# One Strassen level in the up projection of a gated feed-forward, and the gated result kept in DRAM

## The chip, the cores and the metric

The kernel runs on one core of one Trainium2 chip. The metric is device time in microseconds of one execution; times below are medians of separate runs, and the trace is that of one further, profiled execution.

## The reference

An encoder layer is applied with the same weights to 256 prompt tokens and 1024 sample tokens (D = 1024, all float32). The first half (projections, retention, pooling, memory attention, merge, output projection, residual) isn't touched by the change. The second half is a gated feed-forward with a depthwise convolution over the tokens:

```python
h2 = rmsnorm(x, g_ffn_pre)
u = h2 @ w_up                      # 1024 -> 2 * 2816
u = conv(u, conv_w) + conv_b       # centred, width 3, per channel, per group of tokens
gate, val = split(u)
x = x + rmsnorm((gelu(gate) * val) @ w_down, g_ffn_post)
```

The convolution never reaches from prompt tokens to sample tokens.

## The kernel before

Every float32 operand of a matmul is split in two reduced-precision (`fp32r`) parts: `hilo` lets ScalarE copy the high part and VectorE subtract it from the source to get the low part. `mm3` then issues three matmuls: high x high, high x low, low x high. So each product costs three matmuls, and each operand one ScalarE copy and one VectorE subtraction.

`Weights` is the stream of weight units (128 x 1024) through SBUF in the order of a list. SP loads a unit into one of two raw buffers (`wr`), `split_to` splits it into a ring of four pairs `wh`, `wl`, and the buffer's next load is issued then, when the buffer has been read. `take` hands units out and splits ahead up to the ring's limit; `tick` loads and splits when there is room.

Instructions run on each engine in the order in which the program writes them. `bg` is a list of background generators (closing a tile of the output projection, for example); `step` advances each by one piece, so a piece stands in the engines' queues where the main loop calls `step`.

After the output projection (order written out by hand over 10 token tiles and 8 blocks; `finish` writes normalized, transposed activations to DRAM as `h2_d`), the feed-forward runs twice, once for each half of the 1280 tokens. In each half:

- Up: for each of the 22 blocks m of 128 channels, the gate and the value unit of `w_up` are taken. The half's tokens come in two groups (256 + 386 columns in the first, 322 + 322 in the second; the excess columns are neighbours that the convolution needs). Each group and unit is 8 x 3 matmuls into a bank `f`. `conv` reads the bank: ScalarE the centre tap with bias into `z`, VectorE the two outer taps. ScalarE applies GELU and VectorE multiplies gate and value into `gs[m]`, which stays in SBUF.
- Down: 44 steps n, each with the split `gl` of one `gs` block held as TensorE's weights for five token tiles and 512 columns of `w_down` moving.

So `w_up` is read twice. GpSimd does no arithmetic in these stages; it only issues stores. Its queue and SP's are in order too.

Of the kernel before, what the change touches and what calls it, by code (L numbers as in the profile page):

```python
# [8 lines left out]
F32 = mybir.dt.float32  # L9
# [48 lines left out]
class Weights:  # L58
    RAW, RING = 2, 4

    def __init__(self, nc, pool, srcs):
        self.nc, self.pool, self.srcs = nc, pool, srcs
        self.raw, self.hl = {}, {}
        self.n_load = self.n_split = self.n_taken = self.n_done = 0
        self.limit = self.load_limit = len(srcs)

    def load(self):
# [16 lines left out]
    def split_to(self, h, l):  # L84
        r = self.raw.pop(self.n_split)
        self.nc.scalar.activation(h, r[:], AF.Copy)  # L86
        self.nc.vector.tensor_tensor(out=l, in0=r[:], in1=h.bitcast(F32), op=ALU.subtract)  # L87
        self.n_split += 1
        self.load()
# [20 lines left out]
def encoder(ctx: ExitStack, tc: tile.TileContext, a: dict):  # L110
# [3 lines left out]
    dram = ctx.enter_context(tc.tile_pool(name="scratch", bufs=1, space=DRAM))  # L114
    wpool = ctx.enter_context(tc.tile_pool(name="w", bufs=1))
    big = ctx.enter_context(tc.tile_pool(name="big", bufs=1))
# [72 lines left out]
    srcs += [a["w_ret_out"][i] for i in range(8)]  # L189
    srcs += [a["w_o"][i] for i in range(8)]  # L190
    for _ in range(2):
        for p in range(NF):
            srcs += [a["w_up"][p], a["w_up"][NF + p]]
        srcs += [a["w_down"][i] for i in range(NF)]
    ws = Weights(nc, wpool, srcs)
    wo_at = len(srcs) - 2 * 3 * NF - KC
    ws.limit = wo_at
# [27 lines left out]
    x2_d = [dram.tile([P, D], F32, name=f"x2d{i}") for i in range(NT)]  # L225
    h2_d = dram.tile([P, KC, T], F32, name="h2d")

    bg = []
# [702 lines left out]

    slots["bx"] = ctx.enter_context(tc.tile_pool(name="bx", bufs=1))
    op = ctx.enter_context(tc.tile_pool(name="outp", bufs=1))
# [105 lines left out]

    lp = accs.enter_context(tc.tile_pool(name="lhs", bufs=1))  # L1040

    def finish(t, bs, x):
# [23 lines left out]
        for hf in range(2):  # L1066
            b = fbank()[:].rearrange("p (a b) -> p a b", b=P)
            for i in range(4):
                c = 4 * hf + i
                nc.tensor.transpose(b[:, i, :], v[:, c * P:(c + 1) * P], ident[:])  # L1070
            s = op.tile([P, 4, P], F32, tag="h2s", name="h2s", bufs=2)
            nc.scalar.activation(s, b, AF.Copy)
            nc.gpsimd.dma_start(out=h2_d[:, 4 * hf:4 * hf + 4, t * P:(t + 1) * P], in_=s[:])
            yield

    def h2_raw(c, base, r):
        w = min(642, T - base)
        nc.sync.dma_start(out=r[:, 0:w], in_=h2_d[:, c, base:base + w])
        return r[:, 0:w], w

    def h2_split(c, raw):
        r, w = raw
        if c % 2 == 0:
            hx.append(slot([2, 2, 642]))
        s = hx[c // 2]
        hilo(r, s[:, c % 2, 0, 0:w], s[:, c % 2, 1, 0:w], col("g_ffn_pre", c))

    def wraw():
        return wpool.tile([P, 1024], F32, tag="wr", name="wr", bufs=Weights.RAW)

# [22 lines left out]
    for n in range(LA):  # L1113
        acc_split(n)
    hx = []
    raw = {}
    for n, (t, c) in enumerate(order):
# [11 lines left out]
        if t == 0:  # L1129
            if c in (0, 1):  # L1130
                late_merge(c + 1)
            elif c in (2, 3):
                wo += load_wo(1)
            elif c == 4:
                ws.limit = len(srcs)
# [6 lines left out]
        pos = (t - 7) * KC + c  # L1142
        sched = {6: 0, 8: 1, 10: 2, 12: 3, 18: 4, 19: 5, 21: 6, 22: 7}
        if pos in (4, 5):
            raw[pos - 4] = h2_raw(pos - 4, 0, wraw())
        if pos in sched:
            k = sched[pos]
            h2_split(k, raw.pop(k))
            if k + 2 < KC:
                raw[k + 2] = h2_raw(k + 2, 0, wraw())  # L1150
    ws.load_limit = len(srcs)
    accs.close()

    fp = ctx.enter_context(tc.tile_pool(name="ffn", bufs=1))
    gpost2 = []
    halves = (
        (0, 0, ((0, 256, 0, 256), (256, 386, 256, 384))),
        (638, 640, ((639, 322, 640, 320), (958, 322, 960, 320))),
    )

    def conv(b, s, n, o, m, u, first, last):
        z = fp.tile([P, 384], F32, tag=f"z{u}", name="z", bufs=2)
        wi = 3 * (u * NF + m)
        ce = o - s
        nc.scalar.activation(z[:, 0:n], b[:, ce:ce + n], AF.Identity, scale=col("conv_w", wi + 1),  # L1165
                             bias=col("conv_b", u * NF + m))
        l = 1 if first else 0
        nc.vector.scalar_tensor_tensor(out=z[:, l:n], in0=b[:, ce + l - 1:ce + n - 1], scalar=col("conv_w", wi),  # L1168
                                       in1=z[:, l:n], op0=ALU.mult, op1=ALU.add)
        r = n - 1 if last else n  # L1170
        nc.vector.scalar_tensor_tensor(out=z[:, 0:r], in0=b[:, ce + 1:ce + 1 + r], scalar=col("conv_w", wi + 2),  # L1171
                                       in1=z[:, 0:r], op0=ALU.mult, op1=ALU.add)
        return z

# [31 lines left out]

    for hb, (base, tok0, groups) in enumerate(halves):
        gs, gls = [], {}
        last = 2 * NF - (8 if hb else 0)

        def g_split(n):
            if n >= 2 * NF:
                return
            if n < last:
                g = fp.tile([P, 2, 640], F32R, tag="gl", name="gl", bufs=3)[:]
            elif n % 2 == 0:
                gls["pair"] = slot([2, 2, 640])
                g = gls["pair"][:, 0]
            else:
                g = gls["pair"][:, 1]  # L1220
            hilo(gs[n % NF], g[:, 0, :], g[:, 1, :])
            gls[n] = g

        for m in range(NF):
            if m % 4 == 0:
                gt = slot([min(4, NF - m), 640], F32)
            gs.append(gt[:, m % 4, :])
            w2 = ws.take(2)
            if m == NF - 1:
                for k in range(2):  # L1230
                    g_split(k)
            for s, wd, o, n in groups:
                zz = []
                for u in range(2):
                    b = fbank()
                    wh, wl = w2[u]
                    so = s - base
                    for c in range(KC):
                        cs = slice(c * P, (c + 1) * P)
                        x = hx[c // 2][:, c % 2]  # L1240
                        mm3(b[:, 0:wd], wh[:, cs], wl[:, cs], x[:, 0, so:so + wd], x[:, 1, so:so + wd],
                            c == 0, c == KC - 1)
                    zz.append(conv(b, s, n, o, m, u, o in (0, TP), o + n in (TP, T)))
                    ws.tick()
                nc.scalar.activation(zz[0][:, 0:n], zz[0][:, 0:n], AF.Gelu_apprx_tanh)
                nc.vector.tensor_tensor(out=gs[m][:, o - tok0:o - tok0 + n], in0=zz[0][:, 0:n],
                                        in1=zz[1][:, 0:n], op=ALU.mult)
                step()
        while bg:
            step()  # L1250
        if hb == 0:
# [5 lines left out]

        def product(i, n, w):
            k, gl = n % NF, gls[n]
            ts = slice(i * P, (i + 1) * P)  # L1260
            cs = slice((k % 2) * 512, (k % 2 + 1) * 512)
            mm3(bs[i], gl[:, 0, ts], gl[:, 1, ts], w[0][:, cs], w[1][:, cs], k == 0, k == NF - 1)

        for n in range(2 * NF):
# [5 lines left out]
            if n % 2 == 0 and n < last:  # L1270
                w, = ws.take()
            elif n == last:
                held_w = ws.take((2 * NF - last) // 2)
            g_split(n + 2)
            if n < last:
                for i in range(5):
                    product(i, n, w)
# [4 lines left out]
            if hb == 0 and n >= 24 and n % 2 == 0:  # L1282
                k = (n - 24) // 2
                if k == 0:
                    hx = []
                if 1 <= k <= KC:
                    h2_split(k - 1, raw.pop(k - 1))
                if k < KC:
                    raw[k] = h2_raw(k, halves[1][0], xtile())
        if hb:  # L1290
            xs = [load_x2(5 + i) for i in range(3)]
        for i in range(5):
            for n, w in held:
                product(i, n, w)
            last_half(i, 1, bs[i], res, ss)
# [93 lines left out]
```

## Time and profile before

| | |
|---|---|
| median of 3 runs | 2756.62 us (2755.66 to 2758.01) |
| span of the profiled execution | 2753.4 us, 3.2 us under the runs' median |
| TensorE busy | 2731.1 us (99%) |
| VectorE, ScalarE, GpSimd busy | 1341.4, 886.2, 176.1 us |
| up projection, two stages | 1816.5 to 2130.6 and 2280.4 to 2594.3 us |
| down projection, two stages | 2130.7 to 2280.3 and from 2594.4 us |

The span runs from the first instruction to the last. The times of the runs also hold what lies around the span, so the two are compared by their distance. Busy shares are means over the whole span; the stages are read with the table of stages.

### The profile page before, as it was taken

The numbers are of one execution on the slowest core, as the hardware profiler recorded it, in microseconds if no ns is written. First come the engines' busy times: TensorE is split into PE (matmuls) and PEld (weight loads), VectorE is DVE, ScalarE is ACT, GpSimd is POOL, SyncE is SP. The second block draws the span as 40 slices with busy tenths as digits, with TensorE's granted clock in tenths as the row PEclk, the third lists the DMA queues.
The fourth block names the chain that finished last, engine by engine and source line by source line (L and its number), as shares of the span: only waits on it lengthen the run. The fifth ranks groups of instructions, "written<-read, shape, count | busy, mean of one in ns | idle before, by whom it ended". The sixth has DMA issues, their size and how long they took to land.

```text
span 2753.4 us, 38728 instructions
## 1 busy us (share of the span) xinstructions
PE 2731.1 (99%) x15716; PEld 2436.4 (88%) x15716; DVE 1341.4 (49%) x2403; ACT 886.2 (32%) x1527; POOL 176.1 (6%) x331
## 2 busy tenths in 40 slices
PE   8999999999999999999999999999999999999998
PEld 6989998888888888888888888899999889999987
DVE  5645203446445355555324344665555456555544
ACT  5433312221034233233302112553333343333343
POOL 1100100000011111111100000100000000000000
PEclk9999999999999999999999999999999999999999
DMA  7622222222245445444434433442222234222223
GB/s 252 218 79 69 81 85 104 73 74 83 88 145 181 144 141 161 149 141 140 156 105 152 128 122 117 159 140 85 73 67 84 84 117 144 77 77 77 77 77 107
DMA packets 111875, 319.09 MB, mean 116 GB/s; under 512 B 14224, under 2 KB 22544, under 8 KB 111696
## 3 DMA queue, kind: packets, MB, share of 16 engines
q1 hardware_dynamic: 85792, 230.07, 26.1%
q0 software_dynamic: 25616, 86.26, 8.3%
q8 instruction: 124, 2.03, 0.3%
q14 instruction: 55, 0.45, 0.1%
q10 hardware_dynamic: 288, 0.28, 0.0%
HBM read 237.91 MB, written 78.64 MB: 115 GB/s over the span
## 4 chain that ended last, share of the span: by engine, by line
PE 96%; DMA 1%; ACT 1%; DVE 1%; issue 0%; SPq 0%; POOL 0%; DVEq 0%; ACTq 0%; POOLq 0%
PE mm L148 17%; PE mm L146 17%; PE mm L147 17%; PE f L148 12%; PE f L147 12%; PE f L146 12%; PE ch L148 3%; PE ch L147 3%; PE ch L146 3%; DMA wr<-w_kv_in 0%; PE ch L515 0%; PE f L1070 0%; PE ch L886 0%; DMA rel<-rel_in 0%; PE ch L724 0%
## 5 line engine op out<-in xcount | busy, mean ns | idle before, releaser
L148 PE MATMUL mm<-b,wl 128*128 128x512 f32 (+1 forms) x1968 | 703.8, 358 | 0.0
L146 PE MATMUL mm<-b,wh 128*128 128x512 f32 (+1 forms) x1968 | 702.0, 357 | 0.0
L147 PE MATMUL mm<-b,wh 128*128 128x512 f32 (+1 forms) x1968 | 700.5, 356 | 0.0
L146 PE MATMUL f<-b,wh 128*128 128x322 f32 (+2 forms) x1408 | 437.9, 311 | 0.0
L148 PE MATMUL f<-b,wl 128*128 128x322 f32 (+2 forms) x1408 | 437.4, 311 | 0.0
L147 PE MATMUL f<-b,wh 128*128 128x322 f32 (+2 forms) x1408 | 437.2, 311 | 0.0
L147 PEld LDWEIGHTS mm<-b,wh 128*128 128x128 f32 x1968 | 370.0, 188 | 58.4
L148 PEld LDWEIGHTS mm<-b,wl 128*128 128x128 f32 x1968 | 369.8, 188 | 57.5
L146 PEld LDWEIGHTS mm<-b,wh 128*128 128x128 f32 x1968 | 370.1, 188 | 55.5
L87 DVE TENSOR_TENSOR wl<-wr,wh 128x1024 fp32r<-128x1024 f32 x244 | 293.7, 1221 | 221.2 <-ACT wh L86 216.3
L86 ACT ACTIVATE wh<-wr 128x1024 fp32r<-128x1024 f32 x244 | 251.2, 1050 | 283.4 <-PE mm L147 255.2
L147 PEld LDWEIGHTS f<-b,wh 128*128 128x128 f32 x1408 | 267.1, 190 | 0.0
L146 PEld LDWEIGHTS f<-b,wh 128*128 128x128 f32 x1408 | 265.6, 189 | 0.0
L148 PEld LDWEIGHTS f<-b,wl 128*128 128x128 f32 x1408 | 265.6, 189 | 0.0
L1165 ACT ACTIVATE z<-f,pk 128x320 f32<-128x320 f32 (+2 forms) x176 | 108.8, 618 | 390.3 <-PE f L148 390.2
L1168 DVE SCALAR_TENSOR_TENSOR z<-f,pk,z 128x320 f32<-128x320 f32 (+2 forms) x176 | 96.6, 549 | 264.2 <-ACT z L1165 264.2
L148 PE MATMUL f<-wh,gl 128*128 128x512 f32 x400 | 155.6, 389 | 0.0
L146 PE MATMUL f<-wh,gl 128*128 128x512 f32 x400 | 155.6, 389 | 0.0
L147 PE MATMUL f<-wl,gl 128*128 128x512 f32 x400 | 155.6, 389 | 0.0
L919 ACT ACTIVATE gate<-mm 128x512 f32<-128x512 f32 (+1 forms) x68 | 35.6, 524 | 227.2 <-PE mm L148 135.9
L1171 DVE SCALAR_TENSOR_TENSOR z<-f,pk,z 128x255 f32<-128x255 f32 (+3 forms) x176 | 96.9, 551 | 6.2
L139 DVE TENSOR_TENSOR gl<-b,gl 128x640 fp32r<-128x640 f32 x62 | 51.0, 825 | 89.4 <-ACT gl L138 89.4
(296 smaller groups left out, 3974.8 us busy)
## 6 DMA issues: line engine op xcount, KB each, us to landing
wr<-w_up_in SPq DMA_DIRECT2D x88, 512.0 KB, 4.2
wr<-w_in_in SPq DMA_DIRECT2D x72, 512.0 KB, 3.6
wr<-w_down_in SPq DMA_DIRECT2D x44, 512.0 KB, 3.5
h2s<-gtd SPq DMA_DIRECT2D x48, 256.0 KB, 3.7
gtd<-gate POOLq DMA_DIRECT2D x44, 256.0 KB, 2.6
wr<-w_kv_in SPq DMA_DIRECT2D x16, 512.0 KB, 5.7
std<-s POOLq DMA_DIRECT2D x24, 256.0 KB, 3.4
sr<-std SPq DMA_DIRECT2D x24, 256.0 KB, 2.7
```

The lines of the kernel that those rows point to most:

```text
L86: self.nc.scalar.activation(h, r[:], AF.Copy)
L87: self.nc.vector.tensor_tensor(out=l, in0=r[:], in1=h.bitcast(F32), op=ALU.subtract)
L139: nc.vector.tensor_tensor(out=lo, in0=src, in1=hi.bitcast(F32), op=ALU.subtract)
L146: nc.tensor.matmul(out, ah, bh, start=first, stop=False)
L147: nc.tensor.matmul(out, ah, bl, start=False, stop=False)
L148: nc.tensor.matmul(out, al, bh, start=False, stop=last)
L919: nc.scalar.activation(y[:, 0:n], b, AF.Sigmoid)
L1165: nc.scalar.activation(z[:, 0:n], b[:, ce:ce + n], AF.Identity, scale=col("conv_w", wi + 1), bias=col("conv_b", u * NF + m))
L1168: nc.vector.scalar_tensor_tensor(out=z[:, l:n], in0=b[:, ce + l - 1:ce + n - 1], scalar=col("conv_w", wi), in1=z[:, l:n], op0=ALU.mult, op ...
L1171: nc.vector.scalar_tensor_tensor(out=z[:, 0:r], in0=b[:, ce + 1:ce + 1 + r], scalar=col("conv_w", wi + 2), in1=z[:, 0:r], op0=ALU.mult, op ...
```

## The change

The up projection is no longer done by halves of all tokens.

1. Prompt: one pass over the 22 blocks for the 256 prompt tokens with both weight units, as before. Here GpSimd does the subtraction of every second weight unit (`shared`) and the product of gate and value, and issues the store of the result to a new DRAM tile `fg_d[m]`.
2. Meanwhile a generator `h2_terms` reads the normalized sample activations back from DRAM and forms seven operands (`TERMS`): blocks and differences of the 2 x 2 partition of sample activations by contraction half and token half. ScalarE scales, GpSimd subtracts, `hilo` splits. The operands fill eight `big` tiles and one more.
3. Sample: for each q of 22, the gate and the value unit together are partitioned 2 x 2 (output half by contraction half). GpSimd forms four sums and differences in place (`quad_sums`), ScalarE and VectorE split three units and a half (`quad_first`, `quad_s12`, `quad_s34`). Seven products of 4 x 3 matmuls of 512 columns follow (instead of eight); four banks, three of which take a second product, and VectorE additions give gate and value for all 1024 sample tokens, without excess columns. The convolution, GELU and product (`post`, in steps of the next q) work on 1024 columns from SBUF; the result goes to `fg_d[q]`.
4. Down: as before, but its source tiles are loaded from `fg_d` (`g_load`), and both halves of the tokens follow each other directly.

The raw tiles of the Strassen loop come from two pairs, so q+2 loads where q was. The diff, cut:

```diff
+        eng = self.nc.gpsimd if self.shared and self.n_split % 2 else self.nc.vector
+        eng.tensor_tensor(out=l, in0=r[:], in1=h.bitcast(F32), op=ALU.subtract)
...
+    for m in range(NF):
+        w2 = ws.take(2)
+        zz = []
+        for u in range(2):
+            b = fbank()[:, 0:TP]
+            wh, wl = w2[u]
+            for c in range(KC):
+                cs = slice(c * P, (c + 1) * P)
+                mm3(b, wh[:, cs], wl[:, cs], h2p[:, c, 0, :], h2p[:, c, 1, :], c == 0, c == KC - 1)
+            z = hp_p.tile([P, TP], F32, tag=f"zp{u}", name="zp", bufs=2)
+            centre(z, b, u, m)
+            taps(z, b, TP, 3 * (u * NF + m))
+            zz.append(z)
+            ws.tick()
+            step()
+        nc.scalar.activation(zz[0], zz[0][:], AF.Gelu_apprx_tanh)
+        nc.gpsimd.tensor_tensor(out=zz[0], in0=zz[0][:], in1=zz[1][:], op=ALU.mult)
+        nc.gpsimd.dma_start(out=fg_d[m][:, 0:TP], in_=zz[0][:])
...
+    def quad_first(q):
...
+        h, l = unit(r0[:])
+        t = op.tile([P, 2, 512], F32R, tag="x", name="u4", bufs=3)
+        hilo(r1[:, 512:], t[:, 0, :], t[:, 1, :])
...
+    def quad_sums(q):
...
+        for o, x, y, f in ((r0[:, 0:512], r0[:, 0:512], r1[:, 0:512], ALU.subtract),
+                           (r1[:, 0:512], r1[:, 0:512], r1[:, 512:], ALU.add),
+                           (r1[:, 512:], r1[:, 512:], r0[:, 0:512], ALU.subtract),
+                           (r0[:, 512:], r0[:, 512:], r1[:, 512:], ALU.subtract)):
+            nc.gpsimd.tensor_tensor(out=o, in0=x, in1=y, op=f)
...
+    def product(b, w, nm, first, last):
+        for c in range(4):
+            cs = slice(c * P, (c + 1) * P)
+            for k, (x, y) in enumerate(((0, 0), (0, 1), (1, 0))):
+                nc.tensor.matmul(b, w[x][:, cs], hcx[nm, c, y], start=first and c == k == 0,
+                                 stop=last and c == 3 and k == 2, skip_group_check=True)
...
+    def post(q, ug, uv):
+        zg = uz()
+        centre(zg, ug[:], 0, q)
+        taps(zg, ug, TS, 3 * q)
+        yield
+        nc.scalar.activation(zg, zg[:], AF.Gelu_apprx_tanh)
+        yield
+        zv = uz()
+        centre(zv, uv[:], 1, q)
+        yield
+        taps(zv, uv, TS, 3 * (NF + q))
+        yield
+        nc.gpsimd.tensor_tensor(out=zg, in0=zg[:], in1=zv[:], op=ALU.mult)
+        nc.gpsimd.dma_start(out=fg_d[q][:, TP:T], in_=zg[:])
...
+        product(ba, u["A11"], "B11", True, True)
+        us = up.tile([P, HS], F32, tag="us", name="us", bufs=2)
+        nc.scalar.activation(us, ba, AF.Copy)
+        quad_first(q + 1)
+        step()
+        product(bb, u["S2"], "T2", True, True)
+        add(us[:], bb, us[:])
+        quad_sums(q + 1)
+        step()
+        product(ba, u["A12"], "B21", False, True)
+        ug, uv = uz(), uz()
+        nc.scalar.activation(ug[:, 0:HS], ba, AF.Copy)
+        room(2)
+        step()
+        product(bc, u["S1"], "T1", True, True)
+        v = up.tile([P, HS], F32, tag="uv", name="uv", bufs=2)
+        add(v[:], bc, us[:])
+        quad_s12(q + 1)
+        room(3)
+        step()
+        product(bd, u["S3"], "T3", True, True)
+        add(uv[:, HS:TS], bd, v[:])
+        if final:
+            g_load(0, 0)
+        step()
+        product(bc, u["S4"], "B22", False, True)
+        add(ug[:, HS:TS], bc, us[:])
+        quad_s34(q + 1)
+        quad_load(q + 2)
+        room(4)
+        step()
+        product(bd, u["A22"], "T4", False, True)
+        add(uv[:, 0:HS], bd, us[:])
+        bg.append(post(q, ug, uv))
```

## Rows read from the trace of the kernel before

**Rows 1.** The page: busy us, share of the span, instructions by engine.

```profile
PE 2731.1 (99%) x15716; PEld 2436.4 (88%) x15716; DVE 1341.4 (49%) x2403; ACT 886.2 (32%) x1527; POOL 176.1 (6%) x331
```

**Rows 2.** Table of stages: window, busy us (instructions), clock, DMA share, GB/s.

```profile
core 0: us, PE busy (x) PEld busy (x) DVE busy (x) ACT busy (x) POOL busy (x), PEclk, DMA share, GB/s
1816.50:2130.60 314.10, 314.10 (x2127) 314.06 (x2126) 170.12 (x277) 121.12 (x193) 3.56 (x5) 1.00 0.25 83
2130.70:2280.30 149.60, 149.60 (x661) 123.88 (x660) 75.58 (x84) 65.41 (x92) 0.00 (x0) 1.00 0.31 99
2280.40:2594.30 313.90, 313.90 (x2113) 313.90 (x2112) 175.75 (x288) 112.12 (x179) 2.74 (x5) 1.00 0.28 90
```

**Rows 3.** Timeline of TensorE: start, duration, instruction; first and last of two series, last of a third.

```profile
54.75 0.39 PE L147 MATMUL mm<-memT,wh 128*128 128x512 f32 x1
...
61.98 0.40 PE L148 MATMUL ch<-memT,wl 128*128 128x512 f32 x1
...
1831.25 0.28 PE L146 MATMUL f<-b,wh 128*128 128x256 f32 x1
...
1832.32 0.28 PE L146 MATMUL f<-b,wh 128*128 128x256 f32 x1
...
2280.09 0.39 PE L148 MATMUL f<-wh,gl 128*128 128x512 f32 x1
```

**Rows 4.** Groups by line and form, ScalarE: busy us, mean ns, idle before.

```profile
L86 ACT ACTIVATE wh<-wr 128x1024 fp32r<-128x1024 f32 x244 | 251.2, 1050 | 283.4 <-PE mm L147 255.2 <-DMA wr<-w_kv_in 12.4 <-PE f L148 9.8
...
L138 ACT ACTIVATE gl<-b 128x640 fp32r<-128x640 f32 x62 | 45.5, 738 | 107.4 <-PE f L148 107.4
...
L1165 ACT ACTIVATE z<-f,pk 128x384 f32<-128x384 f32 x44 | 29.6, 672 | 143.5 <-PE f L148 143.5
...
L1165 ACT ACTIVATE z<-f,pk 128x256 f32<-128x256 f32 x44 | 24.8, 564 | 45.2 <-PE f L148 45.2
...
L1072 ACT ACTIVATE h2s<-f 128x512 f32<-128x512 f32 x20 | 11.9, 595 | 20.6 <-PE f L1070 20.6
...
L1245 ACT ACTIVATE z<-z 128x384 f32<-128x384 f32 x22 | 11.3, 513 | 0.0
...
L1245 ACT ACTIVATE z<-z 128x256 f32<-128x256 f32 x22 | 9.0, 409 | 2.1 <-DVE z L1171 2.1
```

**Rows 5.** Groups by line and form, VectorE.

```profile
L87 DVE TENSOR_TENSOR wl<-wr,wh 128x1024 fp32r<-128x1024 f32 x244 | 293.7, 1221 | 221.2 <-ACT wh L86 216.3
L139 DVE TENSOR_TENSOR gl<-b,gl 128x640 fp32r<-128x640 f32 x62 | 51.0, 825 | 89.4 <-ACT gl L138 89.4
...
L139 DVE TENSOR_TENSOR qkvhl<-qkvr,qkvhl 128x512 fp32r<-128x512 f32 x60 | 37.8, 685 | 7.3 <-ACT qkvhl L138 7.3
...
L1055 DVE SCALAR_TENSOR_TENSOR x<-x,rqy 128x1024 f32<-128x1024 f32 x10 | 12.8, 1279 | 0.0
...
L996 DVE TENSOR_TENSOR acc<-mm,h2s 128x512 f32<-128x512 f32 x16 | 11.0, 690 | 59.9 <-PE mm L148 59.9
```

**Rows 6.** Groups by line and form, GpSimd: a store's issue, and its arithmetic.

```profile
L1056 POOL DMA_DIRECT2D x2d<-x x10 | 5.5, 551 | 397.8 <-DVE lh L139 360.4 <-DVE x L1055 37.4
...
masks.py:199 POOL TENSOR_SCALAR_AFFINE_SELECT ident<-ident 128x128 f32<-128x128 f32 x1 | 0.3, 289 | 0.1
masks.py:197 POOL MEMSET ident<- 128x128 f32 x1 | 0.2, 205 | 0.3 <-POOLq L1380 0.3
...
L1380 POOL MEMSET const-float32-1.0<- 128x1 f32 x1 | 0.1, 99 | 0.0
```

**Rows 7.** Instructions on the raw weight tile, 1825 to 1900 us: loads to landing.

```profile
DMA to landing us min/median/max: 3.5/4.0/5.7
```

**Rows 8.** Table of stages around a fall of the clock.

```profile
60.00:68.00 8.00, 4.17 (x24) 3.31 (x22) 5.18 (x8) 5.44 (x10) 2.19 (x4) 0.94 0.88 327
68.00:80.00 12.00, 11.68 (x78) 11.69 (x79) 5.88 (x17) 2.96 (x4) 3.75 (x7) 0.76 0.89 318
```

**Rows 9.** Timeline of ScalarE where the first down stage ends.

```profile
2280.57 0.60 ACT L1177 ACTIVATE junk<-f 128x512 f32<-128x512 f32 x1
```

More of the change, by code (lines that the diff above doesn't have):

```diff
@@ L226, in encoder @@
     h2_d = dram.tile([P, KC, T], F32, name="h2d")
+    fg_d = [dram.tile([P, T], F32, name=f"fgd{i}") for i in range(NF)]
     bg = []
@@ L1073, in finish @@
             nc.gpsimd.dma_start(out=h2_d[:, 4 * hf:4 * hf + 4, t * P:(t + 1) * P], in_=s[:])
+            if hf:
+                finished.append(t)
             yield
[L1076 to L1089, printed above, removed]
     LA = 3
@@ L1114, in encoder, with h2_prompt @@
         acc_split(n)
-    hx = []
-    raw = {}
+    hps = ExitStack()
+    hp_p = None
+    h2p = None
+    def h2_prompt():
+        t = hp_p.tile([P, KC, 2, TP], F32R, name="h2p")
+        for k in range(2):
+            r = hp_p.tile([P, D], F32, tag="hr", name="hr", bufs=3)
+            rv = r[:].rearrange("p (a b) -> p a b", b=TP)
+            nc.sync.dma_start(out=rv, in_=h2_d[:, 4 * k:4 * k + 4, 0:TP])
+            for i in range(4):
+                c = 4 * k + i
+                hilo(rv[:, i, :], t[:, c, 0, :], t[:, c, 1, :], col("g_ffn_pre", c))
+        return t
     for n, (t, c) in enumerate(order):
@@ L1155, in encoder @@
-    gpost2 = []
[L1156 to L1173, printed above, removed]
+        if (t, c) == (NT - 1, KC - LA - 1):
+            accs.close()
+            hp_p = hps.enter_context(tc.tile_pool(name="hp", bufs=1, reuse_waits="tile"))
+            h2p = h2_prompt()
@@ new lines, in encoder, with h2_slots @@
+    ws.load_limit = down_at
+    ws.shared = True
+    rights.close()
+    hcs = ExitStack()
+    hc = hcs.enter_context(tc.tile_pool(name="hc", bufs=1, side="right", reuse_waits="tile"))
+    HS = TS // 2
+    TERMS = ("B11", "T2", "B21", "T1", "T3", "B22", "T4")
+    hcx = {}
+    def h2_slots():
+        ts = [big.tile([P, SLOT], F32R, tag="b", name="b", bufs=8) for _ in range(8)]
+        tx = hc.tile([P, 16, HS], F32R, name="hc")
+        for j, nm in enumerate(TERMS):
+            for c in range(KC // 2):
+                for w in range(2):
+                    i = 8 * j + 2 * c + w
+                    hcx[nm, c, w] = ts[i // 5][:, (i % 5) * HS:(i % 5 + 1) * HS] if i < 40 else tx[:, i - 40, :]
@@ new lines, in encoder, with quad_load @@
+    while bg:
+        step()
+    ws.shared = False
+    hps.close()
+    ups = ExitStack()
+    up = ups.enter_context(tc.tile_pool(name="up", bufs=1, reuse_waits="tile"))
+    qraw, qu = {}, {}
+    def quad_load(q):
+        if q < NF:
+            pool, tag = (wpool, "wr") if q % 2 == 0 else (up, "wr2")
+            qraw[q] = [pool.tile([P, 1024], F32, tag=tag, name=tag, bufs=2) for _ in range(2)]
+            for r, i in zip(qraw[q], (q, NF + q)):
+                nc.sync.dma_start(out=r, in_=a["w_up"][i])
@@ new lines, in add, with g_load @@
+    def add(o, x, y):
+        nc.vector.tensor_tensor(out=o, in0=x, in1=y, op=ALU.add)
+    halves = (0, 640)
+    gsl = {}
+    def g_load(hb, k):
+        n = min(4, NF - 4 * k)
+        t = big.tile([P, SLOT], F32, tag="b", name="b", bufs=8)
+        for i in range(n):
+            v = t[:, i * 640:(i + 1) * 640]
+            nc.sync.dma_start(out=v, in_=fg_d[4 * k + i][:, halves[hb]:halves[hb] + 640])
+            gsl[hb, 4 * k + i] = v
+    quad_load(0)
+    quad_first(0)
+    quad_sums(0)
@@ L1175, in last_half @@
+    ws.limit = len(srcs)
+    while bg:
+        step()
+    ups.close()
+    hcs.close()
+    fp = ctx.enter_context(tc.tile_pool(name="ffn", bufs=1, reuse_waits="tile"))
+    gpost2 = []
     def last_half(i, hf, b, res, ss):
@@ L1205, in close_first @@
             yield
-    for hb, (base, tok0, groups) in enumerate(halves):
-        gs, gls = [], {}
+    NS = (NF + 3) // 4
+    loaded = {0: 1, 1: 0}
+    for hb in range(2):
+        gls = {}
         last = 2 * NF - (8 if hb else 0)
@@ L1256, in encoder, with partial @@
         held = []
-        def product(i, n, w):
+        def partial(i, n, w):
             k, gl = n % NF, gls[n]
@@ L1281, in encoder @@
             ws.tick()
[L1282 to L1289, printed above, removed]
+            step()
         if hb:
```

167 lines of the change are left out of this document (113 added, 54 removed).

## The prediction, made before the changed kernel was run

> **What bounds the kernel now.** I read the page first: TensorE is busy for 99% of the span [rows 1], at full clock in the stages that matter here [rows 2], so the time is the sum of what TensorE does. The table of stages [rows 2] says where this change lands: the two passes of the up projection take 314.1 and 313.9 us, TensorE is busy in all of both, and the two passes of the down projection are the other half. In the up stages VectorE is busy for 170 to 176 us and ScalarE for 112 to 121: both hide behind TensorE with room to spare, and the DMA engines are a quarter used. So a column less through TensorE is time saved, as long as the other engines still keep up. That is the question here, because the change takes columns away and adds work to everyone else.
>
> Durations of single matmuls overlap, so I price a matmul from start to start [rows 3]: 256 columns take 0.1189 us (1831.25 to 1832.32, nine steps), 512 columns with a weight tile held take 0.2332 us (54.75 to 61.98, 31 steps). The down projection does its 660 matmuls of 512 columns in 149.6 us [rows 2], 0.2267 each; that is the lower bound for the new products.
>
> **What goes and what comes on TensorE.** Up now: 628.0 us in the two stages [rows 2]. They hold 4240 instructions where 2 x 2112 belong to up; the other 16 (transposes of `finish`) stay and cost about 1.5 us: 626.5 us. After: prompt, 22 x 2 x 8 x 3 = 1056 matmuls of 256 columns x 0.1189 = 125.6 us; Strassen, 22 x 7 products x 4 x 3 = 1848 matmuls of 512 columns x 0.2332 = 431.0 us. Together 556.6, so 69.9 us saved (82 with 0.2267).
>
> **Feeding the prompt pass.** One m of the prompt takes TensorE 5.7 us and needs two weight units. Before, two units had to last 14.3 us. `Weights` has two raw buffers, and a buffer is free for its next load only when the subtraction has read it. Each buffer therefore turns over in landing + ScalarE copy + subtraction. Landing is 4.0 us here [rows 7], the copy 1.05 [rows 4]. The even unit's subtraction is on VectorE, 1.22 [rows 5]: 6.3 us. The odd unit's moves to GpSimd. The trace has no two-input operation there, so I bound it: below by VectorE's 1.22, above by twice that. To choose, GpSimd's small rows [rows 6]: a memset costs 0.1 fixed and (0.205 - 0.099)/128 = 0.83 ns an element; a select that also reads one operand 1.48 ns; one operand's read is thus 0.65 ns, and with two 2.13 ns: an estimate of 2.28 us for 1024 and 1.19 for 512. Its buffer turns over in 4.0 + 1.05 + 2.28 = 7.33 us, longer than 5.7. So this buffer, not TensorE, sets the pace. Four units are split ahead; the odd unit for m = 2 is ready about 5.7 + centre 0.56 + GELU 0.41 + two copies 2.05 + 2.28 = 11.0 us after the start, the one for m = 21 after 19 more turns, 150.3, and its 24 matmuls take 2.85: the pass ends at 153.1, **27.5 us** late (6.3 with 1.22 us). What stands in the queues beside it is covered while the turns are that long: ScalarE needs per m two copies, two centres and a GELU, 3.6 of 7.3 us, and the Strassen terms add 36 actions over 12 m (eight scalings of 1.05, 28 copies of 512 at about 0.6 [rows 4]), 2.1 us per m. GpSimd's multiply and store of one m stand in front of the next odd subtraction, about 1.2 us, inside the wait for its load; the four 512 subtractions of each term group (4.8) are almost hidden too. SP's added loads of normalized x wait for nothing that TensorE needs next.
>
> **The Strassen loop.** Seven products of 2.80 us, 19.6 us per q. Totals per q are small: VectorE three 1024 splits, one 512 split, five additions of 0.69 and four taps of 1.28 = 12.9 us; ScalarE about 8.3; GpSimd 4 x 1.19 + 2.28 + 0.55 = 7.6. But the queues are in order, and the seventh product accumulates in the bank that the addition after the fifth must have read. The chain to that addition, from the end of product one [rows 4, 5]: copy 0.60, copy of the next weights 1.05, subtractions 1.22 and 0.69, two taps 2.56, GELU 1.03 (0.41 and 0.51 at 256 and 384 elements, carried on to 1024), copy 0.60, centre 1.2 (same way from 0.56 and 0.67), copy 1.05, subtraction 1.22, two taps 2.56, addition 0.69: 14.5 us, with hand-overs 14.6. Products two to six last 13.99. So TensorE waits 0.6 us per q, **12.6 us** in 21 (nothing, if the hand-overs and overlaps cancel). The raw weights of q+2 have a whole iteration of time: hidden.
>
> **Where the stages meet.** At the start of Strassen nothing of q = 0 is ready: ScalarE ends the last prompt m (0.56 + 0.41), then copy 1.05 and subtraction 1.22; two of three first matmuls run ahead: 2.8 us lost. Product two waits for three GpSimd sums (3.57), a copy and a subtraction, ready 9.08 us after the prompt's end, 3.0 more than product one covers: **5.8 us** together. At the end, the last q's work stands in front of the first split for down: addition 0.69, taps 2.56, GELU 1.03, centre 1.2, taps 2.56, subtraction 0.83, less 0.47: **8.4 us**; before, the gated value went straight from a tile and this was covered. Between the two down passes, where the up pass used to stand: the last square ends at 2281.17, its last matmul started at 2280.09 [rows 9, 3], then copy 0.74 and subtraction 0.83 [rows 4, 5]: **2.2 us**. The prompt's first split behind the last output-projection tiles: **1 us** (0 to 4.5: eight copies of 0.56 with or without cover). TensorE's clock fell once in this trace after a stretch in which it was busy for 4.2 of 8.0 us: 0.76 over the next 12 us [rows 8], which is 5.8 us at 1.2 GHz, a loss of **3 us**. I charge it once, for the 8.4 us hole (0 to 6). The stores and loads of the gated values add some 96 GB/s to the 99 of the down stage [rows 2]; 318 to 327 GB/s flowed at the beginning [rows 8], so I cost them at nothing; without that cover, a late load would stop TensorE two splits later.
>
> **The sum.** 69.9 saved, less 27.5 + 12.6 + 5.8 + 8.4 + 2.2 + 1 + 3 = 60.5: 9.4 us faster. The profiled span is 2753.4 us, 3.2 below the median of the runs, 2756.6; I take the same distance: 2744.0 in the profile, **2747.2 us**. My likeliest case has its own range of 2733 to 2758.
>
> **The rivals.** *The other side: VectorE and GpSimd shut each other out.* GpSimd's four sums become ready just when VectorE's first taps of the loop run; both read two operands from SBUF. If each of the two taps must wait for one sum, the chain grows by 2 x 1.19 us per q, x 21 = 50.0: **2797 us**. It decides from 0.45 us per q on. For it: the chain has no slack at all. Against: nothing in this trace, where GpSimd never reads SBUF beside VectorE. The Trainium skill, SBUF — State Buffer, "Who interferes with whom", states just this rule: a VectorE instruction with two SBUF inputs and a GpSimd instruction that reads SBUF exclude each other, whole instructions at a time. No row here bears it out or refutes it. GPSIMD Engine Reference, section 3.1, gives 4497 ns for 2048 elements, an estimate of 2.25 us for 1024; by it the feeding term would be 27, as by the rows.
>
> *The hand-over is cheap.* GpSimd subtracts at VectorE's 1.22 us and the loop's chain just fits: 21.2 + 12.6 + 1.5 less waiting, **2712 us**, with 0.2267 us per matmul 2700. For it: successive instructions overlap a little.
>
> *Loads land late.* With both buffers in flight beside stores and the term loads, landing is the 5.7 us maximum [rows 7]: 19 x 1.7 = 32 us more, **2779 us**. For it: landing here varies from 3.5 to 5.7. Against: the DMA engines stay far below what they moved at the beginning.
>
> *No change:* a milder exclusion, in which VectorE goes first and the sums end later: some 0.6 us per q, 13 us, **2760 us**.
>
> **How the numbers follow.** Likeliest 0.42, cheap hand-over 0.21, exclusion 0.20, late loads 0.09, no change 0.08. Less than about 0.2% (5.5 us) can't be told from no change. Of the likeliest case some 0.33 lies below 2751, 0.07 within, the rest above: faster 0.54, same 0.14, slower 0.32. Both bounds are real mechanisms, so the range spans them: 2704 to 2799.
>
> **What the profile would show.** Matmuls into `f` with 256 and 512 columns, 0.119 and 0.233 us apart. In the prompt pass TensorE idle once per m, waiting for GpSimd's `wl`, some 7.3 us per m. In the Strassen loop one wait per q before the seventh product, on VectorE's addition into `uz`; with exclusion, taps or sums visibly longer than 1.28 and 1.19 us. Holes of about 6 and 8 us where the stages meet. Wrong would make it: an odd subtraction far from 2.28 us, landing far from 4, a chain that stretches, or the clock falling in the prompt pass.

## The result, and the profile after

The changed kernel takes 2862.22 us (median of four runs, 2860.03 to 2865.49) against 2757.32 for the kernel before on the same chip: ratio 1.0384, 95% interval 1.0370 to 1.0399. It is slower by 105 us; 2747.2 was forecast.

The page of the kernel after, busy us by engine; the line that answers to [rows 1]:

```profile
PE 2730.1 (95%) x14396; PEld 2320.6 (81%) x14396; DVE 1446.8 (51%) x2293; ACT 920.8 (32%) x1509; POOL 505.0 (18%) x543
```

1320 matmuls fewer, and TensorE is busy as long as before: its busy time hides a slower clock. So the stages come next. The table of stages of the kernel after (prompt pass, Strassen loop, both down passes to the end), with the columns of [rows 2]:

```profile
core 0: us, PE busy (x) PEld busy (x) DVE busy (x) ACT busy (x) POOL busy (x), PEclk, DMA share, GB/s
1814.60:2011.00 196.40, 148.07 (x1071) 141.66 (x1069) 111.13 (x150) 101.78 (x158) 108.84 (x83) 0.90 0.47 154
2011.00:2526.00 515.00, 465.86 (x1848) 367.43 (x1848) 333.09 (x284) 171.48 (x199) 220.27 (x132) 0.93 0.21 70
2526.00:2859.80 333.80, 314.45 (x1320) 250.05 (x1320) 161.11 (x212) 120.67 (x177) 8.29 (x11) 0.98 0.41 139
```

| stage | predicted, us | measured, us | off |
|---|---|---|---|
| prompt pass | 125.6 + 27.5 + 1 + 1.5 (transposes) = 155.6 | 196.4 | +40.8 |
| Strassen loop with its start | 431.0 + 12.6 + 5.8 = 449.4 | 515.0 | +65.6 |
| down, to the end | 308.7 (before) + 8.4 + 2.2 + 3 = 322.3 | 333.8 | +11.5 |

The three differences add up to 117.9. The stage begins 1.9 us earlier than in [rows 2], which leaves 116; the profiled span, 2859.8, is 115.8 above the forecast 2744.0.

**Prompt pass.** The waits of TensorE, then of ScalarE, in this stage (us in total, times, longest):

```profile
PE f L148 <- ACT wh L87: 26.4, 9, 8.1
PE f L150 <- DVE wl L89: 11.9, 12, 2.0
PE f L150 <- POOL wl L89: 8.1, 7, 1.9
```

```profile
ACT wh L87 <- DMA wr<-w_up_in: 33.9, 17, 5.2
ACT hr L1190 <- DMA hr<-h2d: 31.7, 5, 8.4
ACT b L140 <- POOL hr L1202: 14.1, 8, 2.9
```

TensorE waits for 46.4 us, and the longest waits are not for GpSimd's `wl` but for ScalarE's `wh`. ScalarE in turn stands for 31.7 us behind five loads of normalized x. One of them, in the timelines of ScalarE and of SP's queue:

```profile
1890.98 1.15 ACT L1190 ACTIVATE hr<-hr,pk 128x1024 f32<-128x1024 f32 x1 [7.44 <-DMA hr<-h2d]
1892.04 0.40 ACT L1240 ACTIVATE zp<-zp 128x256 f32<-128x256 f32 x1
1892.34 1.04 ACT L87 ACTIVATE wh<-wr 128x1024 fp32r<-128x1024 f32 x1
```

```profile
1882.16 4.20 SPq L71 DMA_DIRECT2D wr<-w_up_in  x2
1886.42 0.90 SPq L1178 DMA_DIRECT2D hr<-h2d  x2
```

The load of `hr` is issued at 1886.42, behind two weight loads that stood on SP until their raw buffers had been read; ScalarE is idle for 7.44 us until 1890.98, and the next weight copy stands behind that. Of the 7.44 us, 2.9 pass before the load is issued and some 4.5 until it has landed: it is also asked for too shortly before its use.

The third of ScalarE's waits, 14.1 us, is for the subtractions by which GpSimd forms the operands of h2. Groups of this stage by line and form:

```profile
L89 POOL TENSOR_TENSOR wl<-wr,wh 128x1024 fp32r<-128x1024 f32 x20 | 48.1, 2404 | 21.8 <-ACT wh L87 21.5
L89 DVE TENSOR_TENSOR wl<-wr,wh 128x1024 fp32r<-128x1024 f32 x20 | 29.2, 1460 | 39.3 <-ACT wh L87 39.3
L1202 POOL TENSOR_TENSOR hr<-hr 128x512 f32<-128x512 f32 x16 | 23.1, 1446 | 0.9
L141 DVE TENSOR_TENSOR b<-hr,b 128x512 fp32r<-128x512 f32 x20 | 22.9, 1162 | 8.9 <-ACT b L140 8.5
```

GpSimd's (L1202) take 1.45 us each where 1.19 was estimated, and VectorE's subtractions of 512 columns take 1.16 us on average, partly beside GpSimd's work, where [rows 5] have 0.69.

The clock falls where the waits are. Around them, from 1857.6 to 1960 us, the granted clock is 0.80 on average:

```profile
1857.60:1960.00 102.40, 71.92 (x458) 68.77 (x459) 63.67 (x75) 55.13 (x84) 59.37 (x43) 0.80 0.46 151
```

A mean of 0.80 between the two levels, 2.4 and 1.2 GHz, is 2 x 0.20 x 102.4 = 41 us at 1.2 GHz, some 20 us lost. TensorE's busy time says the same: 148.1 us where 125.6 and 1.5 for the transposes were priced. Together 46.4 + 20 = 66 of the 70.8 us that the pass takes beyond its 125.6.

**Strassen loop.** TensorE's one large wait between 2030 and 2526 us:

```profile
PE f L1301 <- DVE uz L1323: 46.9, 20, 2.4
```

Once per q, at the place that the prediction named: the seventh product waits for the addition out of its bank. What is in front of that addition, in the timelines of VectorE and GpSimd:

```profile
2299.35 1.23 DVE L141 TENSOR_TENSOR wl<-wr,wh 128x1024 fp32r<-128x1024 f32 x1 [3.67 <-ACT wh L140]
2300.49 0.68 DVE L141 TENSOR_TENSOR u<-wr,u 128x512 fp32r<-128x512 f32 x1
2301.09 2.32 DVE L1216 SCALAR_TENSOR_TENSOR uz<-uz,pk 128x1023 f32<-128x1023 f32 x1
2303.45 2.20 DVE L1218 SCALAR_TENSOR_TENSOR uz<-uz,pk 128x1023 f32<-128x1023 f32 x1
2305.57 0.68 DVE L1323 TENSOR_TENSOR us<-f,us 128x512 f32<-128x512 f32 x1
```

```profile
2300.66 1.67 POOL L1285 TENSOR_TENSOR wr<-wr,wr 128x512 f32<-128x512 f32 x1 [7.77 <-DVE wl L141]
2302.41 2.16 POOL L1285 TENSOR_TENSOR wr<-wr 128x512 f32<-128x512 f32 x1
2304.64 3.55 POOL L1285 TENSOR_TENSOR wr<-wr,wr 128x512 f32<-128x512 f32 x2
```

The two taps take 2.32 and 2.20 us beside GpSimd's sums; an instruction of this kind and size took 1.28 before [rows 5]. The addition behind them, which reads one operand from a bank and one from SBUF, takes its 0.68 us although the sums still run. And after 18 of these 20 waits the clock falls; the window from 2291.1, just behind one wait, and the rest of that q show it:

```profile
2294.50:2315.00 20.50, 18.15 (x78) 14.39 (x77) 13.71 (x13) 7.77 (x9) 9.02 (x5) 1.00 0.18 57
2291.10:2294.50 3.40, 3.40 (x9) 2.64 (x8) 1.98 (x1) 0.00 (x0) 1.50 (x2) 0.50 0.32 124
```

Over the loop's 515 us a mean clock of 0.93 is 2 x 0.07 x 515 = 72 us at 1.2 GHz, 36 us lost: some 3 at the loop's start (the granted clock is 0.51 from 2011 to 2018 us), the other 30 or so behind the waits. Waits, clock and the start account for the loop within a few us: 431 + 46.9 + 36 + 3.9 = 518 for 515.

**Down.** The two holes at the ends of stages came as forecast; the first one:

```profile
2532.16 0.80 PE L148 MATMUL f<-wh,gl 128*128 128x512 f32 x1 [6.20 <-ACT gl L140]
...
2534.91 0.80 PE L150 MATMUL f<-wh,gl 128*128 128x512 f32 x1 [1.52 <-DVE gl L141]
```

But the matmuls themselves got slower at full clock: 430 of 512 columns in 100 us, one or two of which cross an edge of the window, so about 100/428.5 = 0.2333 us each, where [rows 2] give 0.2267. The change also moves the pool of weight tiles to the other end of SBUF (`side="right"` in its code), which neither the list of the change nor the prediction mentions; two of the experiments are about that.

```profile
2560.00:2660.00 100.00, 100.00 (x430) 80.43 (x430) 44.62 (x48) 37.63 (x53) 0.00 (x0) 1.00 0.39 133
```

### The profile page after: what moved, and what is told of

Same layout as the page of the kernel before. It is cut to its first block, busy times and chain, and to the rows that moved or that the text cites. A ratio compares the mean times of both kernels' runs of the same rounds, so it can differ in the third digit from the quotient of the medians.

```text
span 2859.8 us, 36328 instructions
## 1 busy us (share of the span) xinstructions
PE 2730.1 (95%) x14396; PEld 2320.6 (81%) x14396; DVE 1446.8 (51%) x2293; ACT 920.8 (32%) x1509; POOL 505.0 (18%) x543
## 3 DMA queue, kind: packets, MB, share of 16 engines
q1 hardware_dynamic: 92032, 244.47, 26.5%
## 4 chain that ended last, share of the span: by engine, by line
PE 77%; DVE 9%; ACT 4%; DMA 4%; issue 4%; POOL 1%; SPq 0%; DVEq 0%; ACTq 0%; POOLq 0%
PE mm L150 16%; PE mm L148 16%; PE mm L149 16%; PE f L1301 6%; PE f L150 5%; PE f L149 5%; PE f L148 4%; DVE uz L1218 2%; PE ch L150 2%; PE ch L148 2%; PE ch L149 2%; DVE uz L1216 2%; ACT wh L140 1%; DMA wr<-w_up_in 1%; DVE wl L141 1%
## 5 line engine op out<-in xcount | busy, mean ns | idle before, releaser
L87 ACT ACTIVATE wh<-wr 128x1024 fp32r<-128x1024 f32 x200 | 208.5, 1051 | 320.0 <-PE mm L149 255.8
L1301 PE MATMUL f<-b,wh 128*128 128x512 f32 x880 | 278.8, 398 | 2.8 <-ACT wh L140 2.8
L1301 PEld LDWEIGHTS f<-b,wh 128*128 128x128 f32 x880 | 168.0, 191 | 43.5 <-ACT wh L140 3.7
L1301 PE MATMUL f<-b,wl 128*128 128x512 f32 x440 | 174.9, 398 | 1.1 <-DVE wl L141 1.1
L1301 PE MATMUL f<-hc,u 128*128 128x512 f32 x264 | 94.2, 526 | 46.9 <-DVE uz L1323 46.9
L148 PE MATMUL f<-h2p,wh 128*128 128x256 f32 x352 | 106.7, 303 | 26.5 <-ACT wh L87 26.4
L141 DVE TENSOR_TENSOR gl<-b,gl 128x640 fp32r<-128x640 f32 x80 | 67.7, 852 | 125.6 <-ACT gl L140 125.6
L150 PE MATMUL f<-h2p,wl 128*128 128x256 f32 x352 | 107.3, 305 | 20.1 <-DVE wl L89 11.9
L1301 PEld LDWEIGHTS f<-hc,u 128*128 128x128 f32 x264 | 66.6, 259 | 72.2 <-DVE uz L1323 55.7
L1285 POOL TENSOR_TENSOR wr<-wr 128x512 f32<-128x512 f32 x55 | 101.0, 1837 | 87.6 <-DVE wl L141 84.1
L140 ACT ACTIVATE gl<-b 128x640 fp32r<-128x640 f32 x80 | 58.6, 738 | 169.7 <-PE f L150 163.4
```

The costliest lines, as they stand in the source:

```text
L140: nc.scalar.activation(hi, src, AF.Copy)
L141: nc.vector.tensor_tensor(out=lo, in0=src, in1=hi.bitcast(F32), op=ALU.subtract)
L148: nc.tensor.matmul(out, ah, bh, start=first, stop=False)
L150: nc.tensor.matmul(out, al, bh, start=False, stop=last)
L1285: nc.gpsimd.tensor_tensor(out=o, in0=x, in1=y, op=f)
L1301: nc.tensor.matmul(b, w[x][:, cs], hcx[nm, c, y], start=first and c == k == 0, stop=last and c == 3 and k == 2, skip_group_check=True)
```

## The experiments

The variants have one run each, but for the last two; runs of the kernel before on their chips took 2754.4 to 2755.1 us. Differences to the kernel after are against 2862.2.

### Who stretches the taps, and what falls with the clock

Four variants of the kernel after, each with one edit in the Strassen loop.

```diff
 # e2_sums_vector, in quad_sums
-            nc.gpsimd.tensor_tensor(out=o, in0=x, in1=y, op=f)
+            nc.vector.tensor_tensor(out=o, in0=x, in1=y, op=f)
 # e3_sums_memset, the same line
+            nc.gpsimd.memset(o, 0.5)
 # e4_filler, before the seventh product
+        for i in range(10):
+            nc.tensor.matmul(bb, u["A22"][0][:, 0:P], hcx["T4", 0, 0], start=True, stop=True,
+                             skip_group_check=True)
 # e8_own_bank: the seventh product gets the free bank bb, at the price of one more addition
         add(uv[:, HS:TS], bd, v[:])
+        add(uv[:, 0:HS], bd, us[:])
...
-        product(bd, u["A22"], "T4", False, True)
-        add(uv[:, 0:HS], bd, us[:])
+        product(bb, u["A22"], "T4", True, True)
+        add(uv[:, 0:HS], bb, uv[:, 0:HS])
```

e3_sums_memset leaves the four sums out and writes a constant in their place.

e2_sums_vector. 

> The four sums of each q move from GpSimd to VectorE, nothing else. Theory (two-operand reads of VectorE and GpSimd exclude each other, and the late seventh product then drops the clock): the taps go back from 1.70 to 1.75 us to about 1.28, the loop's period falls from 23.9 us to 20.2 if the clock stays up (2784 us in all) or to about 22 if the remaining wait of some 0.6 us still drops it (2820). Rival (VectorE's total work bounds the loop): 2.8 us more work per q makes it longer, some 2920.

e3_sums_memset. 

> GpSimd writes a constant in place of each of the four sums, so the sums are left out of the computation; order, places and waits stay. Theory (exclusion needs a read on GpSimd's side): a write alone doesn't hold VectorE up, the taps take 1.28 us, the period is 20.2 to 22 us, 2784 to 2820. Rival (any GpSimd access to SBUF slows VectorE, or the taps are slow for another reason, such as where their operands lie): the taps stay above 1.6 us and the time near 2862.

e4_filler. 

> Ten matmuls of 512 columns (2.3 us) into a bank that nobody reads any more are put in front of the seventh product; they use the time in which TensorE waits. Theory (the clock falls because of that wait, and the fall costs some 1.7 us per q): the loop's period falls from 23.9 to about 22.2 us although TensorE does more, 2825 us in all. Rival (the clock's falls are not caused by this wait, or cost nothing): 2862 or later, as the added work takes its own time.

e8_own_bank. 

> The seventh product goes to the bank of the second, which is free by then, and VectorE adds one 512 addition per q; so no product waits for the late addition. Theory (the chain through VectorE's queue to that one bank sets the period): TensorE's waits in the loop go, the clock stays up, the period is 19.6 to 20 us, 2775 us in all, although the taps stay long. Rival (VectorE and GpSimd together, excluding each other, have no room left in 20 us): the wait turns up at another product and the time stays above 2830.

Measured: 2801.92, 2789.57, 2840.75 and 2786.82 us. First the taps, groups by line and form in the loop: the kernel after, the sums on VectorE, and GpSimd writing without reading.

```profile
L1216 DVE SCALAR_TENSOR_TENSOR uz<-uz,pk 128x1023 f32<-128x1023 f32 x42 | 74.4, 1772 | 3.9 <-ACT uz L1222 3.9
```

```profile
L1216 DVE SCALAR_TENSOR_TENSOR uz<-uz,pk 128x1023 f32<-128x1023 f32 x42 | 53.7, 1278 | 3.9 <-ACT uz L1222 3.9
```

```profile
L1216 DVE SCALAR_TENSOR_TENSOR uz<-uz,pk 128x1023 f32<-128x1023 f32 x42 | 53.7, 1278 | 3.9 <-ACT uz L1222 3.9
...
L1285 POOL MEMSET wr<- 128x512 f32 x80 | 38.4, 523 | 134.1 <-DVE wl L141 116.1 <-issue 17.9
```

GpSimd in the same place, but writing only, leaves the taps at 1278 ns; with the sums they take 1772 on average (half of them run beside sums). So GpSimd's reading is needed for it; on VectorE's side the addition above, with one operand in SBUF, was not held up. That agrees with the Trainium skill, SBUF — State Buffer, "Who interferes with whom": an instruction of VectorE with two SBUF inputs contends with one of GpSimd that reads SBUF, not with one that only writes it.

Then TensorE's wait in the loop: 46.9 us in the kernel after, 11.1 with the sums on VectorE (20 times, longest 0.9), 8.0 with the memset (longest 0.4), none with the filler or the own bank. The same window of the loop in five kernels, in this order: after, sums on VectorE, memset, filler, own bank.

```profile
2060.00:2440.00 380.00, 342.45 (x1365) 271.05 (x1364) 247.93 (x210) 126.14 (x147) 164.00 (x96) 0.94 0.20 68
```

```profile
2060.00:2440.00 380.00, 369.94 (x1575) 294.14 (x1574) 297.72 (x320) 148.22 (x171) 53.52 (x36) 1.00 0.23 78
```

```profile
2060.00:2440.00 380.00, 372.36 (x1584) 295.70 (x1584) 255.68 (x247) 144.82 (x168) 93.11 (x114) 1.00 0.23 77
```

```profile
2060.00:2440.00 380.00, 379.95 (x1618) 302.16 (x1617) 265.63 (x223) 132.00 (x153) 176.19 (x104) 1.00 0.22 73
```

```profile
2060.00:2440.00 380.00, 380.00 (x1639) 307.43 (x1638) 299.07 (x274) 150.69 (x175) 197.91 (x116) 1.00 0.24 79
```

The filler does 10 useless matmuls per q (its taps are as long as before, 1.77 us over the loop) and the kernel is 21.5 us faster: matmuls that compute nothing in place of the wait hold the clock at 1.00. So the clock is a cost of its own, behind the wait. (22 x 10 fillers at 380/1617 = 0.235 us are 52 us, 5 more than the waits they replace; so the gain stays under the 30 us that the clock cost there.) The own bank shows the whole: 1639 matmuls against 1365 in 380 us, with exclusion and long taps still there (1.77 us over the loop), because nothing on TensorE waits for them any more. In time the filler and the own bank came out 16 and 12 us above what was expected, and the sums on VectorE between their two cases.

### What starves the prompt pass

```diff
 # e5_terms_later, in h2_terms after load(c + 5)
+                yield
+                yield
 # e6_raw4, in Weights.load: from m = 5 on odd units load into two more raw tiles
+            if self.more and self.n_load % 2:
+                t = self.more.tile([P, 1024], F32, tag="x", name="x", bufs=3)
 # e7_prompt_vector
-    ws.shared = True
+    ws.shared = False
-                nc.gpsimd.tensor_tensor(out=o, in0=x, in1=y, op=ALU.subtract)
+                nc.vector.tensor_tensor(out=o, in0=x, in1=y, op=ALU.subtract)
 # e9_prompt: e6, e7, loads of h2 on GpSimd's queue, and more steps between load and use
-            nc.sync.dma_start(out=r, in_=h2_d[:, c, TP:T])
+            nc.gpsimd.dma_start(out=r, in_=h2_d[:, c, TP:T])
```

e5_terms_later. 

> The kernel after with two more steps between a load of h2 and its use. Theory A (in the prompt pass ScalarE stands behind h2 loads that SyncE issued too late, 31.7 us in five waits): the five waits fall to under 10 us together, the prompt pass from 196 to about 165 us or less, half clock there from 41 us to under 20; about 2830 us. Theory B (odd units' raw buffer turns over too slowly, whatever h2 does): the waits for h2 go, waits for weights take their place, and the prompt pass stays within 10 us of 196; 2855 to 2862 us.

e6_raw4. 

> The kernel after with four raw buffers for weights in place of two from the sixth tile of the prompt pass on. Theory B (raw buffers turn over too slowly): the waits of TensorE for weight splits in the prompt pass go from 46 us to under 15, no half clock, the pass takes 140 to 155 us; about 2815 us. Theory A (the h2 loads alone): the queue still blocks ScalarE at the h2 steps, the pass stays over 175 us; about 2845 us.

e7_prompt_vector. 

> The kernel after with no two-operand work of GpSimd in the prompt pass apart from the gated product: the odd units' subtraction and the sums of h2 on VectorE. Theory that GpSimd's slow subtraction and its exclusion with VectorE feed the pass late: each subtraction 1.22 us instead of 2.40, raw buffers come free earlier, the pass falls to 140 to 160 us, about 2815 us. Rival (VectorE is then itself too busy, or the h2 loads decide): the pass stays over 180 us, about 2850 us.

e9_prompt. 

> The kernel after with the four feeds of the prompt pass mended at once: h2 loads on GpSimd's queue and issued earlier, all subtractions on VectorE, four raw buffers for weights. Theory A+B (each of the three alone moved the end by 10 to 19 us because each left the other stalls and the half clock in place): no wait of ScalarE for h2, no half clock, the pass falls from 196 us to 130 to 145; about 2800 us. Rival (ScalarE and VectorE have too much to do in the pass, whatever the order): the pass stays over 165 us; over 2825 us.

Measured, with ScalarE's two waits for loads and TensorE's waits in the pass (the pass from its first to its last matmul, 194.3 us in the kernel after):

| kernel | us | pass | ScalarE for `hr` | ScalarE for `wr` | TensorE for `wh`, `wl` |
|---|---|---|---|---|---|
| after | 2862.2 | 194.3 | 31.7 | 33.9 | 46.4 |
| e5_terms_later | 2847.78 | 180.8 | 9.0 | 42.9 | 35.9 |
| e6_raw4 | 2852.05 | 180.3 | 26.5 | 5.8 | 34.3 |
| e7_prompt_vector | 2843.62 | 176.8 | 31.1 | 19.4 | 36.1 |
| e9_prompt | 2819.75 | 150.5 | 5.5 | 4.4 | 18.0 |

Each theory held for its own wait and missed the time: earlier `hr` loads take away the wait for `hr` and ScalarE then waits for weights; more raw buffers take away the wait for weights and leave that for `hr`. Either one alone still starves TensorE. e7_prompt_vector, with the largest gain of the three, leaves ScalarE's waits for `hr` as they were (31.1 us), so those are not the whole of it either. Mended together, the pass falls by 43.8 us. It does not come to the 130 to 145 expected, and the second half of it in e9_prompt says why:

```profile
1876.10:1967.00 90.90, 80.47 (x668) 78.63 (x666) 85.77 (x123) 62.95 (x100) 26.59 (x33) 1.00 0.57 196
```

The clock is full, and VectorE is busy for 85.8 of 90.9 us. TensorE's only waits in this stretch are eight for VectorE's splits, 10.3 us in all. With GpSimd relieved, VectorE limits the pass; its subtractions of 512 columns for the operands of h2, 1.16 us in the kernel after, take 0.74 here. Some of the rival was right.

### The slower matmuls of the down stages

Two variants of the kernel before, each with one pool at the other end of SBUF.

```diff
 # e1_wpool_right
-    wpool = ctx.enter_context(tc.tile_pool(name="w", bufs=1))
+    wpool = ctx.enter_context(tc.tile_pool(name="w", bufs=1, side="right"))
 # e11_gl_right
-    fp = ctx.enter_context(tc.tile_pool(name="ffn", bufs=1))
+    fp = ctx.enter_context(tc.tile_pool(name="ffn", bufs=1, side="right"))
```

e1_wpool_right. 

> The kernel before with the pool of weight tiles moved to the other end of SBUF and nothing else. Theory that the addresses of the weights cost TensorE time in the down stages: 0.232 us for each 512-column matmul there instead of 0.2267, 1320 times, about 6 to 8 us, so about 2762 us. Rival (the longer period of the down stages comes from the new order of work): no change, 2755 us within 2 us.

e11_gl_right. 

> The kernel before with the pool of the FFN stages (split gated result, residuals) at the other end of SBUF and the weights where they were. Theory (what sets the down stages' matmul period of 0.2267 or 0.2333 us is how weights and split gated result lie to each other, which is why putting the weight pool back in the repaired kernel did not bring 0.2267 back): period 0.233, about 2762 us. Rival (only the place of the weights counts, and the repaired kernel is slower there through its DMA traffic of 133 GB/s against 107): period 0.2267, 2755 us.

Measured: 2762.48 and 2765.05 us, 8.1 and 10.6 above the kernel before on the same chips. One hundred us of the first down stage, in the kernel before, e1_wpool_right and e11_gl_right (TensorE, clock, DMA share, GB/s):

```profile
2150.00:2250.00 100.00, 100.00 (x443) 1.00 0.29 91
```

```profile
2150.00:2250.00 100.00, 100.00 (x431) 1.00 0.27 91
```

```profile
2150.00:2250.00 100.00, 100.00 (x430) 1.00 0.27 91
```

Moving either the weights or the split gated result costs 12 or 13 matmuls in 100 us, at the same clock and with the same traffic (91 GB/s each). So in the kernel before it is neither the order of work nor the DMA; it is where the two operands lie. (Moving the weights can shift the pools that were placed behind them as well.) That the same sets the period in the changed kernel is likely, since it has the weight pool at that end, but not shown. Which addresses go together well was not found out.

### Mended together

e10_noearly is e9_prompt with the own bank, the weight pool at its old end, and the first two splits of `gl` issued ahead of the last tile's elementwise work, into a tile of `big`; the load that they need is issued two products earlier. e10_all also loads and splits the first tile of the Strassen loop during the last prompt tile.

```diff
+    early = big.tile([P, SLOT], F32R, tag="b", name="b", bufs=8)
...
+    for k in range(2):
+        hilo(gsl[0, k], early[:, k, 0, :], early[:, k, 1, :])
     while bg:
         step()
```

e10_noearly. 

> That, with a bank of its own for the seventh product, the weight pool back at its old end of SBUF, and the first two splits of the gated result before the last tile's elementwise work. Sum: 2787 for the bank alone, less 55 for the prompt pass, 8 for the matmul period of the down stages, 8 to 10 for the start of the down stage: about 2715 us (2700 to 2735), faster than before's 2755. If the gains overlap: 2740 or more.

e10_all. 

> That, and the first tile of the Strassen loop loaded and split during the last prompt tile. About 4 to 7 us less than without it (waits of 5.9 us and 3 us of half clock at the start of the loop); if the prompt tail is then the later one, no difference.

Measured: 2740.25 us (ratio to the kernel before 0.9941, interval 0.9927 to 0.9956) and 2740.18 us (0.9938, 0.9922 to 0.9955). Both beat both kernels, by 15 us over the kernel before and 122 over the one after. Over the kernel before that is 0.6%, clear of the noise but small. The earlier start of the loop makes no difference. 2715 was expected. The stages of e10_noearly:

```profile
1814.70:1966.00 151.30, 131.37 (x1069) 127.68 (x1068) 123.84 (x184) 99.20 (x155) 41.88 (x55) 0.97 0.58 198
1966.00:2406.00 440.00, 434.05 (x1852) 349.61 (x1851) 333.98 (x308) 174.24 (x203) 221.07 (x132) 0.99 0.25 83
2406.00:2738.00 332.00, 311.53 (x1320) 248.43 (x1319) 158.95 (x212) 119.44 (x176) 7.80 (x11) 0.99 0.41 140
```

The prompt pass takes what it took in e9_prompt (151.3, 150.5), the loop 440.0 us against 515.0. The down stages, where some 17 us were expected, got nearly nothing, 332.0 against 333.8. Their matmuls stayed slow with the weights at their old end (430 in 100 us here too; e11_gl_right was made to see that). And the hole moved: the first two splits are early, the third now comes late.

```profile
2422.20 0.79 PE L152 MATMUL f<-wh,gl 128*128 128x512 f32 x1 [7.88 <-ACT gl L144]
```

## Why the prediction was wrong

**What bounds the kernel** and **what goes on TensorE** were right. With its waits gone (own bank), the loop ran at 380/1637.5 = 0.2321 us per matmul where 0.2332 was assumed. The saved columns are real: e10 turns what is left of them into a gain.

**Feeding the prompt pass** failed first at this sentence: "SP's added loads of normalized x wait for nothing that TensorE needs next." It asked what these loads wait for, and not what waits for them: they stand behind weight loads that wait for a buffer and then need some 4.5 us to land, ScalarE stands behind them, and its weight copies behind ScalarE. That is 31.7 us of ScalarE's time, but not the whole: e5_terms_later leaves 9.0 of it, and its pass still takes 180.8 us. The second wrong step is that the four subtractions of each term group are "almost hidden too": ScalarE waits 14.1 us for them. The parts of the raw buffer's turn were about right: the landing took 3.7 us where 4.0 was taken, GpSimd's subtraction 2.40 where 2.28 was estimated, VectorE's 1.46 where 1.22 was taken. By the Trainium skill, GPSIMD Engine Reference, section 3.1, an estimate for GpSimd's would have been 2.25 us, half of its 4497 ns for 2048 elements; the 2.40 measured here are 7% longer. All that was put beyond the pass's 125.6 us was 30.0 (27.5, the first split and the transposes); it measured 70.8, of which some 20 are clock.

**The Strassen loop** had its wait at the right place and its bare size nearly right: 12.6 us were forecast, and 8.0 were left when GpSimd only wrote. The failed step is that the sum priced the taps at 1.28 us while GpSimd's sums stood beside them, and left the exclusion to a rival at 0.20. That rival's mechanism is what happened: the two taps grew by 1.04 and 0.92 us, and the waits by 46.9 - 8.0 = 39 us where it gave 50. It too missed the clock: some 30 us more behind the waits, which no case contained. "Totals per q are small" was true, but totals say nothing about which pairs meet in time.

**Where the stages meet** was right in each place: 5.8 forecast and 3.9 measured at the start of the loop, 8.4 and 7.7 at the end, 2.2 and 3.2 between the down passes. Only **the clock** was wrong, "charged once" at 3 us: it fell in the prompt pass (20), in the loop (36, nearly all behind its waits) and in the down stages (2 x 0.02 x 333.8 = 13 us at 1.2 GHz, some 7 lost). [Rows 8] were read as a price for one hole; the rows after show that a wait of 2.35 us per q is followed by a fall at nearly every q, and that waits of 0.4 to 0.9 us (memset, sums on VectorE) are not.

**Down stages at 0.2267** was carried over from the kernel before without asking what it rests on. In the kernel before it rests on where the operands lie, and the change moves the weight pool. That the period of 0.2333 in the changed kernel has this cause is argued; its size is measured, 1320 x 0.0066 = 8.7 us of the 11.5 that this part was off.

The range reached to the exclusion alone, 2799. The exclusion with its clock, a late prompt pass and its clock together go past it. Exclusion and a later feed had been kept as alternatives, each with all the rest as forecast; both happened at once, though the later feed did not come from slow landings as its rival had it, and the clock came on top.

What stays open: how much of the prompt pass belongs to each of the four edits (they act on each other), which addresses slow the matmuls (and whether they alone do so in the changed kernel), and whether the third split's wait in e10 can be hidden too, which was not tried.

## What to carry to other kernels

When work moves to an idle engine, look at which instructions it will run beside, not at totals, and price a VectorE instruction with two operands in SBUF beside a GpSimd instruction that reads SBUF as if in series (here taps of 1.28 us took 2.32 and 2.20). For each added instruction in an in-order queue ask both questions, what it waits for and who stands behind it. Where TensorE is the bound, a small regular wait can cost much of its length again through the clock (here 46.9 us of waits, some 30 of clock): give the waiting product a bank of its own first, since that lets everything behind it be late.

## What the runs showed of the hardware

- A wait of 2.35 us in every 23.9 us was enough to bring the granted clock to 1.2 GHz at nearly each q (18 of 20); ten matmuls of no use in its place kept 2.4 GHz and gained 21.5 us.
- In the down stage of the kernel before, the period of matmuls of 512 columns depends on where weight tiles and split gated result lie in SBUF: 443 against 430 or 431 in 100 us, with one pool put at the other end and nothing else edited.
- GpSimd's subtraction of 1024 columns takes 2.40 us, its sums of 512 columns 1.71 to 1.89 us beside VectorE; a memset of 512 columns takes 0.52 us and leaves VectorE's taps beside it at 1.28 us.
